# A transformer block's input projection: half of its contraction by one Strassen level, and indexer scores at full array height

## The chip, the cores and the metric

The kernel runs on 1 core of one Trainium2 chip. The metric is the device time of one execution in microseconds (us), here the median of three runs. TensorE multiplies matrices out of SBUF into PSUM (8 banks of 128 x 512 floats); VectorE and ScalarE compute on SBUF and PSUM; GpSimd and SyncE mostly issue DMAs. SBUF has 128 partitions.

## The reference

x is 512 tokens of 4096 features, all float32. The block computes

```
h  = RMSNorm(x) * pre_norm
z  = h @ w_in                       # 4096 -> 9808 columns, split into:
     q 2048 | c 512 | qi 1024 | k_idx 64 | w_idx 16 | gate_a 2048 | pool_in 2048 | gate_b 2048
c  = RMSNorm(c); k_idx = LayerNorm(k_idx)
I[t,s] = sum over 16 heads of w_idx[t,h] * relu(qi[t,h] . k_idx[s])   # heads of 64 features
top 128 keys per query of I, within admissible 64-token chunks
ya = softmax(q_lat . c_sel / sqrt(128)) . c_sel, 16 heads, mapped by w_uk and w_uv; times silu(gate_a)
yb = (trailing mean over 2/4/8/16 tokens - token) @ w_pool * pool_scale; times silu(gate_b)
out = x + RMSNorm(concat(ya, yb) @ w_out) * post_norm
```

Every large product is done in three matmuls of a reduced-precision format: each operand is split into a high part `hi` (a cast) and a low part `lo` (the rest), and hi*hi + hi*lo + lo*hi is accumulated.

## The kernel before

*Tiling.* h transposed is held in SBUF as 32 contraction tiles of 128 features x 512 tokens, each as a high and a low part (128 KB of a partition's memory). A **group** (function `group`, L254) makes 128 columns of z, transposed: 128 columns x 512 tokens in one PSUM bank. It loops over 8 quarters q of w_in's column block; each quarter is a 256 KB DMA of four 128 x 128 weight tiles, split by `staged` (L69: DMA on SP's queue, cast on ScalarE L66, subtraction on VectorE L67, rings of 4 buffers), and 4 x 3 matmuls (`mm3`, L78 to L82) of 512 columns. A group is 96 matmuls. Two PSUM banks ("acc") alternate between groups; six others ("w") serve everything else. There are 72 groups: 8 for qi, 16 each for pool_in, gate_b, q and gate_a. c, k_idx and w_idx come out of the first stage.

*Order of stages.* (0) L139: x is loaded, scaled and split, with c and k_idx beside it. (1) L298: 8 qi groups of 384 columns (the first 128 queries need no selection); `dots` (L299) makes the indexer scores of a group's two heads for 3 query blocks, each head on 64 of the array's rows (L307), relu on ScalarE, a weighted sum on VectorE. (2) L484: `pool_group` 0 (four pool_in groups with `mixer`, four gate_b groups, the pool map `ymix`); the top-k selection `select` (L335) goes on beside it on VectorE. (3) L492: 16 attention heads: a q group, a gate_a group, and `attn` (L495). (4) L563: `pool_group` 1 to 3. (5) L611: output projection, 20 of 32 contraction tiles by one Strassen level: 8 column blocks x 10 tile pairs = 80 steps; each forms seven weight combinations in `weights` (L384, VectorE and ScalarE), runs 7 products x 2 halves x 3 matmuls of 256 columns (L616 to L621), and after ten steps `collect` (L578) combines the seven products into partial sums, written to DRAM by GpSimd's queue. (6) L680: the remaining 12 tiles directly, added to the partials, norm and residual. Operands of stage 5 are read back from DRAM (`cat`) and formed by `operands` (L368) during the last groups.

*What sets the order.* Background work (dots, select, mixers, pool maps, attention) is written as Python generators in a queue `Bg` (L275) with priorities. `bg.step(per)` runs `per` pieces, one `yield` each; a group calls it after each of its first 7 quarters and once after its evacuation. `bg.drain` runs all that is left. A list scheduler then places the instructions on the engines' queues by this written order, later ones first where an earlier one is not ready or finds no free buffer. A buffer tag with `bufs=1` is taken by the next tile only when all readers of the last one are done; in `attn` these are the keys `kh`, `kl`, the queries `qh`, `ql`, the probabilities `prob` and the scratch `t2`; the gate `sg` has two.

Of the kernel before, what the change touches and what calls it, by code (L numbers as in the profile page):

```python
# [16 lines left out]
P = 128  # L17
# [31 lines left out]
def block_kernel(ctx: ExitStack, tc: tile.TileContext, xT, x, gk, wc, wkw, wf, wuk, wuv, kvn,  # L49
# [4 lines left out]
    big_a = ctx.enter_context(tc.tile_pool(name="big_a", bufs=1))  # L54
    big_stack = ctx.enter_context(ExitStack())
    big_b = big_stack.enter_context(tc.tile_pool(name="big_b", bufs=1))
    st_stack = ctx.enter_context(ExitStack())
    st = st_stack.enter_context(tc.tile_pool(name="st", bufs=4))
# [41 lines left out]
    slots = {}  # L100

    def big(t, shape, name, dt=F32R):
        return (big_b if t < NT else big_a).tile(shape, dt, tag=f"k{t}", name=name)

    def x_slot(i):
        t, j = divmod(i, 7)
        if t not in slots:
            slots[t] = big(t, [P, min(7, 2 * NK - 7 * t), S], f"xk{t}")
        return slots[t][:, j]

    xh, xl = [], []
# [13 lines left out]
    mb = cTp.tile([P, OFF[4]], F32, name="mb")  # L125
# [5 lines left out]
    with tc.tile_pool(name="s0", bufs=2) as s0:  # L131
# [7 lines left out]
        for k2 in range(NK // 2):  # L139
# [20 lines left out]
            for j in range(2):  # L160
# [3 lines left out]
                xh.append(x_slot(2 * k))  # L164
                xl.append(x_slot(2 * k + 1))
# [27 lines left out]
    isc = kixp.tile([P, OFF[4]], F32, name="isc")  # L193
# [60 lines left out]
    def group(gi, evac, per=1, t0=0, before=None, after=None):  # L254
        gis, evacs = (gi, evac) if isinstance(gi, tuple) else ((gi,), (evac,))
        zs = [bank("acc") for _ in gis]
        for q in range(8):
            for i, z in enumerate(zs):
                hi, lo = staged(wf[gis[i], q])
                if before:  # L260
                    before(q, i)
                for j in range(4):
                    k = 4 * q + j
                    mm3(z[:, t0:], (hi[:, ts(j, P)], lo[:, ts(j, P)]), (xh[k][:, t0:], xl[k][:, t0:]),
                        k == 0, k == NK - 1)
                if q < 7:
                    bg.step(per)
            if after:
                after(q)
            if q == 7:  # L270
                for z, evac in zip(zs, evacs):
                    evac(z)
                    bg.step(per)
# [24 lines left out]
    with tc.tile_pool(name="ix", bufs=2, reuse_waits="tile") as ix:  # L298
        def dots(g, qp):  # L299
            for b in range(1, NB):  # L300
                n = P * (b + 1)
                dp = [bank() for _ in range(2)]
                lhs = [sub(qp, slice(64 * j, 64 * j + 64), ts(b, P)) for j in range(2)]
                rhs = [sub(kT, slice(64 * j, 64 * j + 64), slice(0, n)) for j in range(2)]
                for i, (x0, x1) in enumerate(((0, 0), (0, 1), (1, 0))):
                    for j in range(2):
                        nc.tensor.matmul(dp[j][:, :n], lhs[j][x0], rhs[j][x1], start=i == 0, stop=i == 2)  # L307
                yield
                for j in range(2):
                    h = 2 * g + j  # L310
                    r = ix.tile([P, S], F32, name="relu")
                    A.activation(r[:, :n], dp[j][:, :n], AF.Relu)
                    o = isc[:, OFF[b]:OFF[b + 1]]
                    w = wix[:, b, h:h + 1]
                    if h == 0:
                        V.tensor_scalar(o, r[:, :n], w, None, op0=ALU.mult)
                    else:
                        V.scalar_tensor_tensor(o, r[:, :n], w, o, op0=ALU.mult, op1=ALU.add)
                yield

        for g in range(8):
            qp = (ix.tile([P, S], F32R, name="qih"), ix.tile([P, S], F32R, name="qil"))
# [10 lines left out]
    kT_stack.close()  # L333

    def select():  # L335
        V.memset(mb[:, :P], 0.0)
        V.memset(mb[:CHUNK, CHUNK:P], NEG)
        for b in range(1, NB):
            V.memset(isc[:CHUNK, OFF[b + 1] - CHUNK:OFF[b + 1]], INADM)
        yield  # L340
        for r in range(TOPK // 8):
            for b in range(1, NB):
                o = isc[:, OFF[b]:OFF[b + 1]]
# [5 lines left out]
        for b in range(1, NB):  # L349
            V.tensor_scalar(mb[:, OFF[b]:OFF[b + 1]], isc[:, OFF[b]:OFF[b + 1]], -3.2e38, NEG,  # L350
# [17 lines left out]
    def operands(i, pool, tag, bufs, home):  # L368
        w = pool.tile([P, 8, H], F32, tag=tag, name="cw", bufs=bufs)
        q, s = w[:, 0:4], w[:, 4:8]  # L370
        for j in range(2):
            nc.sync.dma_start(q[:, 2 * j:2 * j + 2], cat[i + KA * j].rearrange("p (a t) -> p a t", a=2))
# [5 lines left out]
        o = home([P, 2, 7, H], f"ops{i}")  # L378
        split(w[:, 0:3:2], o[:, 0, 0:2], o[:, 1, 0:2])
        split(w[:, 3:8], o[:, 0, 2:7], o[:, 1, 2:7])  # L380
        ops[i] = o
        yield

    def weights(db, i):  # L384
        w = ow.tile([P, 8, H], F32, tag="wr", name="wr", bufs=2)
        nc.sync.dma_start(w[:, 0:4], wq[i, db].rearrange("p (a c) -> p a c", a=4))
        V.tensor_sub(w[:, 4:6], w[:, 1:3], w[:, 0:2])  # L387
        V.tensor_sub(w[:, 6], w[:, 2], w[:, 4])
        V.tensor_sub(w[:, 7], w[:, 3], w[:, 6])
        hi = ow.tile([P, 7, H], F32R, tag="wh", name="wh", bufs=2)  # L390
        lo = ow.tile([P, 7, H], F32R, tag="wl", name="wl", bufs=2)
        split(w[:, 0:3:2], hi[:, 0:2], lo[:, 0:2])
        split(w[:, 3:8], hi[:, 2:7], lo[:, 2:7])
        return hi, lo
# [4 lines left out]
    def pool_group(pl, pm, g):  # L399
# [22 lines left out]
        for c in range(4):  # L422
            def evac(z, c=c):
# [4 lines left out]
            group(G_PI + 4 * g + c, evac)  # L428
# [7 lines left out]
        def gated(d, yp):  # L436
            def evac(z):
                bg.drain(1)
# [9 lines left out]

        if g < 3:
            for d in range(4):  # L450
                group(G_GB + 4 * g + d, add(d), 2 if d == 0 else 1)
            return lambda: None
        evs = [add(d) for d in range(4)]
        group(G_GB + 4 * g, evs[0], 2)
        bg.drain(1)

        def rest():
            first = []

            def early(q):  # L460
                if q == 3:
                    first.append(operands(0, ow, "wr", 2, lambda sh, n: ex.tile(sh, F32R, name=n)))
                if q in (3, 5):
                    next(first[0])

            group(G_GB + 4 * g + 1, evs[1], after=early)
            cur = []

            def before(q, i):
                if i == 0:  # L470
                    cur[:] = [operands(q, ow, "wr", 2, lambda sh, n: big(q - 1, sh, n))] if q else []
                for e in cur:
                    next(e)

            def after(q):
                if q == 7:
# [3 lines left out]
            group((G_GB + 4 * g + 2, G_GB + 4 * g + 3), (evs[2], evs[3]), before=before, after=after)  # L480
# [11 lines left out]
    with tc.tile_pool(name="at", bufs=1, reuse_waits="tile") as at:  # L492
# [53 lines left out]
        for h in range(NH):  # L546
# [14 lines left out]
    cT_stack.close()  # L561
    right = ctx.enter_context(ExitStack())
    with tc.tile_pool(name="pl1", bufs=1, reuse_waits="tile") as pl:  # L563
        with tc.tile_pool(name="pm1", bufs=1, reuse_waits="tile") as pm:
            for g in range(1, 4):
                rest = pool_group(pl, pm, g)
        ex = right.enter_context(tc.tile_pool(name="ex", bufs=1, side="right", reuse_waits="tile"))
# [3 lines left out]

    inner.close()
    st_stack.close()

    PRODUCTS = ((0, 0), (1, 2), (4, 5), (5, 4), (3, 3), (2, 6), (6, 1))
# [21 lines left out]

    def load_cat(e):
        raw = st.tile([P, S], F32, tag="raw", name="cat_raw")
        nc.sync.dma_start(raw, cat[2 * KA + e])  # L600
        ct[e] = (fin.tile([P, S], F32R, name=f"ch{e}"), fin.tile([P, S], F32R, name=f"cl{e}"))
        split(raw, *ct[e])

    def prefetch(n):
        if n < len(steps) and n not in ahead:
# [3 lines left out]
            ahead[n] = staged(wout[lanes[lane][0], e])  # L609

    for n, (db, i) in enumerate(order):  # L611
# [12 lines left out]
        if db == 0 and i in (0, 1, 3, 4):  # L624
            if i in (0, 3):
                late = [operands(8 + i // 3, oc, "cw", 1, lambda sh, m, t=7 + i // 3: big(t, sh, m))]
            next(late[0])
        if db == 7:
            if i == NT:
                big_stack.close()  # L630
                fin_stack = ctx.enter_context(ExitStack())
                fin = fin_stack.enter_context(tc.tile_pool(name="fin", bufs=1, reuse_waits="tile"))
                st = fin_stack.enter_context(tc.tile_pool(name="st2", bufs=4, reuse_waits="tile"))
            if i > KA - 3:
                prefetch(i - KA + 2)
        if i == KA - 1:
            pt = oc.tile([P, 7, 512], F32, name="pt")
# [12 lines left out]
    def spare(i):  # L650
        t, j = NT + i // 7, i % 7
        if t not in home:
            home[t] = big(t, [P, 7, 512], f"sp{t}", F32)
# [68 lines left out]
def _lay_out(x, pre_norm, w_in, kv_norm, w_uk, w_uv, idx_k_norm_g, idx_k_norm_b, w_pool, pool_scale, w_out,  # L722
# [16 lines left out]
    def quads(m):  # L739
# [6 lines left out]
    inv = np.stack([1.0 / np.minimum(pos, n) for n in WINS]).astype(np.float32).reshape(1, -1)  # L746
    a = {
# [5 lines left out]
        "wf": np.concatenate([groups(part[i]) for i in (2, 6, 7, 0, 5)]),  # L753
# [31 lines left out]
```

## Time and profile before

| | |
|---|---|
| runs shown | 2581.66, 2585.19, 2586.48 us; median 2585.19 |
| profiled execution | 2583.32 us, span from first to last instruction 2581.5 |
| mean granted TensorE clock | 0.997 |
| instructions | 34385, of them 13210 matmuls |
| HBM | 291.43 MB read, 25.17 MB written |

The page gives each engine's busy time and its share of the span (PE: matmuls, PEld: weight loads, DVE: VectorE, ACT: ScalarE, POOL: GpSimd). Matmuls are pipelined: one lasts longer than the distance to the next start, so distances are read from a timeline. A line number may be a helper's (L66, L67, L80 to L82). In a table of windows each row has the stretch and its length, then busy us and number of instructions of PE, PEld, DVE, ACT and POOL, the granted clock (1.00 is 2.4 GHz, 0.50 is 1.2 GHz), the DMA share and GB/s. In a timeline a row has start, duration, engine, line, operation, out<-in, shapes and count; brackets hold the idle time before it and what ended it. In groups by line "| busy us, mean ns of one | idle us before <-what ended it".

### The profile page before, as it was taken

How to read it: one execution, taken by the hardware profiler on the slowest of the kernel's cores; microseconds unless marked ns; L12 is line 12 of the kernel's file. 1: busy time of each engine (PE TensorE's matmuls, PEld its weight loads, DVE VectorE, ACT ScalarE, POOL GpSimd, SP SyncE). 2: the span in 40 equal slices, each digit the busy share in tenths (PEclk: the TensorE clock that was granted, in tenths of full speed). 3: DMA queues.
4: the chain of work that ended last, by engine and by line, in shares of the span. 5: the costliest groups of instructions: out<-in, count | busy, mean ns of one | idle time of the engine just before them, and what ended most of it. 6: DMA issues, size and time to landing. Idle time of an engine off the chain costs nothing.

```text
span 2581.5 us, 34385 instructions
## 1 busy us (share of the span) xinstructions
PE 2549.7 (99%) x13210; PEld 2187.5 (85%) x13210; DVE 1340.4 (52%) x2376; ACT 901.0 (35%) x1558; POOL 13.3 (1%) x28
## 2 busy tenths in 40 slices
PE   9999999999999999999999999999999999999996
PEld 7899888888888888888888888888899999998875
DVE  6465863343444444444344334334687777763447
ACT  6444322232333333333332222222444444443333
POOL 0000000000000000000000000000000000000000
PEclk9999999999999999999999999999999999999998
DMA  8433233322332232323333332332443433476456
GB/s 307 149 111 109 92 102 106 102 91 94 93 96 90 90 97 92 94 91 93 94 94 95 106 106 94 110 102 94 157 130 132 128 117 127 135 248 225 136 174 238
DMA packets 163077, 318.86 MB, mean 124 GB/s; under 512 B 18528, under 2 KB 26848, under 8 KB 162912
## 3 DMA queue, kind: packets, MB, share of 16 engines
q1 hardware_dynamic: 160480, 308.28, 37.5%
q0 software_dynamic: 2432, 8.39, 0.8%
q8 instruction: 103, 1.69, 0.3%
q14 instruction: 62, 0.51, 0.1%
HBM read 291.43 MB, written 25.17 MB: 123 GB/s over the span
## 4 chain that ended last, share of the span: by engine, by line
PE 94%; DVE 3%; DMA 2%; ACT 1%; issue 0%; SPq 0%; DVEq 0%; ACTq 0%
PE ps_acc L80 21%; PE ps_acc L82 20%; PE ps_acc L81 20%; PE ps_w L81 6%; PE ps_w L82 6%; PE ps_w L80 6%; PE ps_w L620 4%; PE ps_w L621 4%; PE ps_w L619 4%; DMA raw<-in_wout 1%; PE ps_w L535 1%; PE ps_w L307 1%; PE ps_acc L621 1%; DMA wr<-in_wq 1%; PE ps_acc L620 1%; PE ps_acc L619 1%
## 5 line engine op out<-in xcount | busy, mean ns | idle before, releaser
L67 DVE TENSOR_TENSOR lo<-raw,hi 128x512 fp32r<-128x512 f32 x776 | 533.6, 690 | 934.6 <-ACT hi L66 861.7
L66 ACT CAST hi<-raw 128x512 fp32r<-128x512 f32 x776 | 482.0, 622 | 1254.8 <-PE ps_acc L81 910.7
L80 PE MATMUL ps_acc<-xk,hi 128*128 128x512 f32 (+1 forms) x2304 | 893.0, 388 | 0.0
L82 PE MATMUL ps_acc<-xk,lo 128*128 128x512 f32 (+1 forms) x2304 | 883.7, 384 | 0.1
L81 PE MATMUL ps_acc<-xk,hi 128*128 128x512 f32 (+1 forms) x2304 | 883.6, 384 | 0.0
L80 PEld LDWEIGHTS ps_acc<-xk,hi 128*128 128x128 f32 x2304 | 432.8, 188 | 81.7 <-issue 2.5
L82 PEld LDWEIGHTS ps_acc<-xk,lo 128*128 128x128 f32 x2304 | 432.5, 188 | 81.6 <-DVE lo L67 0.4
L81 PEld LDWEIGHTS ps_acc<-xk,hi 128*128 128x128 f32 x2304 | 433.0, 188 | 76.1
L620 PE MATMUL ps_w<-wl,ops 128*128 128x256 f32 x960 | 270.4, 282 | 3.2 <-DVE wl L67 3.2
L621 PE MATMUL ps_w<-wh,ops 128*128 128x256 f32 x960 | 270.6, 283 | 0.0
L619 PE MATMUL ps_w<-wh,ops 128*128 128x256 f32 x960 | 268.8, 282 | 0.5 <-DVE sg L363 0.5
L66 ACT CAST wh<-wr 128x512 fp32r<-128x512 f32 (+1 forms) x160 | 145.3, 942 | 223.7 <-PE ps_acc L621 181.0
L67 DVE TENSOR_TENSOR wl<-wr,wh 128x512 fp32r<-128x512 f32 (+1 forms) x160 | 173.8, 1089 | 48.1 <-ACT wh L66 47.4
L620 PEld LDWEIGHTS ps_w<-wl,ops 128*128 128x128 f32 x960 | 181.6, 189 | 4.3 <-DVE wl L67 4.0
L619 PEld LDWEIGHTS ps_w<-wh,ops 128*128 128x128 f32 x960 | 180.2, 189 | 0.7 <-DVE sg L363 0.7
L621 PEld LDWEIGHTS ps_w<-wh,ops 128*128 128x128 f32 x960 | 180.5, 188 | 0.0
L81 PE MATMUL ps_w<-lo,ch 128*128 128x512 f32 x312 | 122.9, 394 | 5.1 <-DVE lo L67 5.0
L80 PE MATMUL ps_w<-hi,ch 128*128 128x512 f32 x312 | 120.9, 392 | 1.9 <-ACT hi L66 1.9
L82 PE MATMUL ps_w<-hi,cl 128*128 128x512 f32 x312 | 121.9, 391 | 0.0
L81 PEld LDWEIGHTS ps_w<-lo,ch 128*128 128x128 f32 x312 | 59.0, 189 | 20.0 <-DVE lo L67 7.9
L80 PEld LDWEIGHTS ps_w<-hi,ch 128*128 128x128 f32 x312 | 58.7, 189 | 15.2 <-ACT hi L66 3.2
L387 DVE TENSOR_TENSOR wr<-wr 128x512 f32<-128x512 f32 x80 | 55.2, 690 | 28.8 <-DMA wr<-in_wq 28.4
(215 smaller groups left out, 2278.3 us busy)
## 6 DMA issues: line engine op xcount, KB each, us to landing
raw<-in_wf SPq DMA_DIRECT2D x576, 256.0 KB, 2.6
wr<-in_wq SPq DMA_DIRECT2D x80, 512.0 KB, 3.6
raw<-in_wout SPq DMA_DIRECT2D x120, 256.0 KB, 3.5
raw<-in_wc SPq DMA_DIRECT2D x32, 256.0 KB, 5.3
xn<-in_x SPq DMA_DIRECT2D x32, 256.0 KB, 4.5
pp<-part SPq DMA_DIRECT2D x32, 256.0 KB, 4.6
xt<-in_xT SPq DMA_DIRECT2D x15, 512.0 KB, 5.5
cw<-cat SPq DMA_DIRECT2D x20, 256.0 KB, 3.0
```

What stands on the lines that cost most here:

```text
L66: A.copy(hi, src)
L67: V.tensor_sub(lo, src, hi.bitcast(F32))
L80: nc.tensor.matmul(dst, lh, rh, start=start, stop=False)
L81: nc.tensor.matmul(dst, lh, rl, start=False, stop=False)
L82: nc.tensor.matmul(dst, ll, rh, start=False, stop=stop)
L307: nc.tensor.matmul(dp[j][:, :n], lhs[j][x0], rhs[j][x1], start=i == 0, stop=i == 2)
L387: V.tensor_sub(w[:, 4:6], w[:, 1:3], w[:, 0:2])
L535: nc.tensor.transpose(tp[:, ts(b - s, P)], prob[:, OFF[b] + P * s:OFF[b] + P * s + P], ident)
L619: nc.tensor.matmul(zz, ab[0], wh[:, w], start=i == 0 and h == 0, stop=False)
L620: nc.tensor.matmul(zz, ab[0], wl[:, w], start=False, stop=False)
L621: nc.tensor.matmul(zz, ab[1], wh[:, w], start=False, stop=i == KA - 1 and h == 1)
```

## The change

*SBUF and order.* x's tiles 0 to 15 live in eight tiles `p0` to `p7` by quadrants (two contraction halves x two halves of the tokens), tiles 16 to 31 in `d0` to `d7`. After the qi groups the first four gate_b groups run in full, interleaved, and their raw results go to DRAM (`zxd`). During the qi groups `d0` to `d7` are copied to DRAM (`xsp`); then x is read again and its sums for Strassen are formed in their place (`build`).

*The new stage.* The 60 remaining groups, in 30 pairs, get contraction tiles 0 to 15 by one Strassen level: per pair 4 steps; a step loads 512 KB, forms seven weight combinations (`form_weights`, the body of the former `weights`), and runs 2 x 7 x 3 matmuls of 256 columns with the weights stationary and x moving. After four steps ScalarE copies four half-filled or full banks and `collect_z` combines them into the pair's partial sums, which GpSimd's queue writes to DRAM (`zpd`). In the last pair `p0` to `p7` are refilled with tiles 16 to 31 from `xsp`. Then the staging rings are opened again on the side where the combination buffers were.

*The direct stages.* `group` now loads a partial sum into one of 8 slots (`d6`, `d7`), runs 16 tiles (4 quarters, 48 matmuls), and adds the partial on VectorE before the old evacuation. Background work is stepped after 3 quarters and once after the evacuation. `pool_group` 0 runs its four pool_in groups interleaved, and its gates (from `zxd`) as background; pool groups 0, 1 and 2 precede attention, 3 follows. After attention the staging rings move to the space that the latent `cTh`, `cTl` and attention's tiles leave. The output's operands are formed in two parts (`sum_part`, `pure_part`), and the tail rotates its buffers within the same tiles; its work is the same.

*The scores.* A head's query high and low parts are stacked on the 128 rows (the other head's rows hold the low part), the keys are there twice already, and a block takes 2 heads x 2 matmuls of 128 rows in place of 2 x 3 of 64.

```diff
 def dots(g, qp):
     for b in range(1, NB):
         ...
-        lhs = [sub(qp, slice(64 * j, 64 * j + 64), ts(b, P)) for j in range(2)]
-        rhs = [sub(kT, slice(64 * j, 64 * j + 64), slice(0, n)) for j in range(2)]
-        for i, (x0, x1) in enumerate(((0, 0), (0, 1), (1, 0))):
-            for j in range(2):
-                nc.tensor.matmul(dp[j][:, :n], lhs[j][x0], rhs[j][x1], start=i == 0, stop=i == 2)
+        for j in range(2):
+            for i in range(2):
+                nc.tensor.matmul(dp[j][:, :n], qp[j][:, ts(b, P)], kT[i][:, :n], start=i == 0, stop=i == 1)
...
 def evac(z, qp=qp):
     ...
-    split(qf[:, P:], *sub(qp, slice(None), slice(P, S)))
+    for j in range(2):
+        o, r = (slice(IDX_D * i, IDX_D * i + IDX_D) for i in (j, 1 - j))
+        split(qf[o, P:], qp[j][o, P:], qp[j][r, P:])
-group(G_QI + g, evac, t0=P)
+stream(wf, (g,), FULL, (evac,), t0=P)
+nc.gpsimd.dma_start(xsp[g], xd[g])
...
+def stream(src, gis, ks, evac, per=1, t0=0, tags=None, before=None, after=None):
+    zs = [bank(t) for t in tags or ["acc"] * len(gis)]
+    for q in range(len(ks) // 4):
+        for i, z in enumerate(zs):
+            hi, lo = staged(src[gis[i], q])
+            ...
+            for j in range(4):
+                k = ks[4 * q + j]
+                mm3(z[:, t0:], (hi[:, ts(j, P)], lo[:, ts(j, P)]), (xh[k][:, t0:], xl[k][:, t0:]),
+                    k == ks[0], k == ks[-1])
+            if 4 * q + 4 < len(ks):
+                bg.step(per)
+        ...
+    for z, e in zip(zs, evac):
+        e(z)
+        bg.step(per)
+def group(gi, evac, per=1, **kw):
+    ...
+        nc.sync.dma_start(parts[-1], zpd[g])
+    def adder(zp, e):
+        def run(z):
+            V.tensor_add(zp, z, zp)
+            e(zp)
+        return run
+    stream(wd, gis, DIRECT, [adder(*a) for a in zip(parts, evacs)], per, **kw)
...
+def collect_z(m, pt):
+    V.tensor_add(pt[:, 1], pt[:, 0], pt[:, 1])
+    V.tensor_add(pt[:, 2], pt[:, 2], pt[:, 0])
+    V.tensor_add(pt[:, 4], pt[:, 4], pt[:, 2])
+    yield
+    V.tensor_add(pt[:, 0], pt[:, 3], pt[:, 4])
+    V.tensor_add(pt[:, 3], pt[:, 3], pt[:, 2])
+    V.tensor_add(pt[:, 3:5], pt[:, 3:5], pt[:, 5:7])
+    yield
+    z = [zpd[2 * m + j].rearrange("p (a t) -> p a t", a=2) for j in range(2)]
+    nc.gpsimd.dma_start(z[0], pt[:, 1:4:2])
+    nc.gpsimd.dma_start(z[1][:, 0], pt[:, 4])
+    nc.gpsimd.dma_start(z[1][:, 1], pt[:, 0])
+    yield
+with tc.tile_pool(name="pa", bufs=2, side="right", reuse_waits="tile") as pa:
+    for n, (m, t) in enumerate(order_s):
+        if t == 0:
+            banks = [bank(b) for b in ("w", "w", "w", "acc")]
+        wh, wl = first.pop(n)
+        for c in range(2):
+            i = 2 * t + c
+            for j, (a, w) in enumerate(PRODUCTS):
+                ...
+                nc.tensor.matmul(zz, w0, x0, start=i == 0 and j % 2 == 0, stop=False)
+                nc.tensor.matmul(zz, w1, x0, start=False, stop=False)
+                nc.tensor.matmul(zz, w0, x1, start=False, stop=last)
+            if m == NPAIR - 1:
+                xd[i] = big(f"p{i}", [P, 2, 2, S], f"xr{i}")
+                nc.gpsimd.dma_start(xd[i], xsp[i])
+                ...
+        if t == NA // 2 - 1:
+            pt = pa.tile([P, 7, H], F32, name="pt")
+            ...
+            bg.add(collect_z(m, pt), 0)
+        if n + 2 < len(order_s):
+            first[n + 2] = s_weights(n + 2)
+        bg.step()
+    bg.drain()
+wa_stack.close()
+st_stack = ctx.enter_context(ExitStack())
+st = st_stack.enter_context(tc.tile_pool(name="st", bufs=4, side="right", reuse_waits="tile"))
...
-    pool_group(pl, pm, 0)
+    for g in range(3):
+        pool_group(pl, pm, g)
     bg.drain()
...
-    group(G_Q + h, evac)
+    group(Q + h, evac)
     sg = at.tile([P, S], F32, tag="sg", name="sga", bufs=2)
     bg.add(attn(h, qp, sg))
-    group(G_GA + h, lambda z, sg=sg: gate(at, z, sg))
+    group(GA + h, lambda z, sg=sg: gate(at, z, sg))
 bg.drain()
 cT_stack.close()
+st_stack.close()
+st = st_stack.enter_context(tc.tile_pool(name="st3", bufs=4, reuse_waits="tile"))
...
-    for g in range(1, 4):
-        rest = pool_group(pl, pm, g)
+    rest = pool_group(pl, pm, 3)
+    bg.drain(3)
```

## Rows read from the trace of the kernel before

**Rows 1.** The page: busy time by engine; the last chain by engine.

```profile
PE 2549.7 (99%) x13210; PEld 2187.5 (85%) x13210; DVE 1340.4 (52%) x2376; ACT 901.0 (35%) x1558; POOL 13.3 (1%) x28
...
PE 94%; DVE 3%; DMA 2%; ACT 1%; issue 0%; SPq 0%; DVEq 0%; ACTq 0%
```

**Rows 2.** Table of windows: output's Strassen stage, direct projection.

```profile
1889.00:2292.00 403.00, 400.99 (x3334) 400.04 (x3334) 321.57 (x460) 178.09 (x226) 11.45 (x21) 1.00 0.42 134
1330.00:1870.00 540.00, 540.00 (x2378) 446.06 (x2377) 227.14 (x376) 146.69 (x233) 0.00 (x0) 1.00 0.34 108
```

**Rows 3.** Timeline of PE, direct projection, 107 steps apart.

```profile
461.98 0.39 PE L80 MATMUL ps_acc<-xk,hi 128*128 128x512 f32 x1
...
486.23 0.39 PE L82 MATMUL ps_acc<-xk,lo 128*128 128x512 f32 x1
```

**Rows 4.** Timeline of PE, output's Strassen stage, 54 steps apart.

```profile
2029.79 0.28 PE L619 MATMUL ps_w<-wh,ops 128*128 128x256 f32 x1
...
2036.27 0.28 PE L619 MATMUL ps_w<-wh,ops 128*128 128x256 f32 x1
```

**Rows 5.** Timeline of PE around one block of indexer scores.

```profile
228.16 0.34 PE L82 MATMUL ps_acc<-xk,lo 128*128 128x384 f32 x1
...
228.42 0.50 PE L307 MATMUL ps_w<-kTh,qih 64*128 64x512 f32 x2
...
229.60 0.33 PE L81 MATMUL ps_acc<-xk,hi 128*128 128x384 f32 x1
```

**Rows 6.** Groups by line and form: weight forming, output stage.

```profile
L67 DVE TENSOR_TENSOR wl<-wr,wh 128x1280 fp32r<-128x1280 f32 x80 | 119.0, 1488 | 15.4 <-ACT wh L66 15.1
...
L66 ACT CAST wh<-wr 128x1280 fp32r<-128x1280 f32 x80 | 101.0, 1263 | 27.7 <-DVE wr L389 27.6
...
L387 DVE TENSOR_TENSOR wr<-wr 128x512 f32<-128x512 f32 x80 | 55.2, 690 | 28.8 <-DMA wr<-in_wq 28.4
...
L67 DVE TENSOR_TENSOR wl<-wr,wh 128x512 fp32r<-128x512 f32 x80 | 55.2, 690 | 32.6 <-ACT wh L66 32.3
...
L66 ACT CAST wh<-wr 128x512 fp32r<-128x512 f32 x80 | 49.6, 620 | 196.0 <-PE ps_acc L621 181.0 <-DMA wr<-in_wq 7.9 <-PE ps_w L621 3.9
...
L388 DVE TENSOR_TENSOR wr<-wr 128x256 f32<-128x256 f32 x80 | 33.7, 422 | 1.3
```

**Rows 7.** Waits (us in total, times, longest), output's Strassen stage.

```profile
PE ps_w L620 <- DVE wl L67: 2.0, 3, 1.1
```

**Rows 8.** DMA issues (count, KB each, us to landing).

```profile
wr<-in_wq SPq DMA_DIRECT2D x80, 512.0 KB, 3.6
...
part<-pt POOLq DMA_DIRECT2D x16, 256.0 KB, 3.2
```

**Rows 9.** Table of windows, attention, from one head's transposes to the next's.

```profile
1218.50:1269.83 51.33, 51.33 (x240) 42.82 (x239) 21.09 (x43) 16.52 (x33) 0.00 (x0) 1.00 0.31 93
```

**Rows 10.** Groups by line and form in the same head's window.

```profile
L67 DVE TENSOR_TENSOR lo<-raw,hi 128x512 fp32r<-128x512 f32 x17 | 11.7, 691 | 23.5 <-ACT hi L66 21.2 <-PE ps_w L535 2.3
...
L514 ACT ACTIVATE prob<-prob,nm 128x512 f32<-128x512 f32 x1 | 0.7, 724 | 1.4 <-DVE nm L511 1.4
...
L511 DVE CUSTOM_DVE_ANT_0 prob<-ps_w,mb 128x512 f32<-128x512 f32 x1 | 0.7, 683 | 0.0
...
L516 DVE TENSOR_SCALAR prob<-prob,sm 128x512 f32<-128x512 f32 x1 | 0.5, 485 | 0.0
```

**Rows 11.** Timeline of PE at the end of attention's last head.

```profile
1324.87 0.82 PE L535 MATMUL ps_w<-ident,prob 128*128 128x128 f32 x6
...
1325.44 0.47 PE L80 MATMUL ps_acc<-xk,hi 128*128 128x512 f32 x1
...
1329.07 0.28 PE L82 MATMUL ps_w<-pth,vl 128*128 128x128 f32 x1
```

**Rows 12.** Timeline of PE behind an idle stretch of the tail.

```profile
2536.92 0.79 PE L81 MATMUL ps_w<-lo,ch 128*128 128x512 f32 x1 [2.71 <-DVE lo L67]
```

**Rows 13.** Table of windows, the two us behind that row.

```profile
2538.00:2540.00 2.00, 2.00 (x6) 1.59 (x5) 2.00 (x5) 0.00 (x0) 0.00 (x0) 0.50 0.90 306
```

More of the change, by code (lines that the diff above doesn't have):

```diff
@@ L252, in block_kernel @@
         split(tp, *kT)
[L254 to L257, printed above, removed]
+    FULL = list(range(2 * NA, NK)) + list(range(2 * NA))
+    DIRECT = FULL[:NK - 2 * NA]
+    def stream(src, gis, ks, evac, per=1, t0=0, tags=None, before=None, after=None):
+        zs = [bank(t) for t in tags or ["acc"] * len(gis)]
+        for q in range(len(ks) // 4):
             for i, z in enumerate(zs):
-                hi, lo = staged(wf[gis[i], q])
+                hi, lo = staged(src[gis[i], q])
                 if before:
@@ new lines, in block_kernel, with before, after @@
+        builds = [e for e in range(NA) for _ in range(2)]
+        gens = {}
+        def before(q, i):
+            if q >= 2 and i % 2 == 0 and builds and not (q > 5 and i):
+                for _ in range(2 if q < 4 else 1):
+                    pass
+            if q >= 2 and builds:
+                e = builds.pop(0)
+                if e not in gens:
+                    gens[e] = build(e)
+                next(gens[e])
+        def after(q):
+            if q == 0:
+                bg.drain()
+                ix_stack.close()
+                kT_stack.close()
+                lend["w1"] = wa_stack.enter_context(tc.tile_pool(name="wa1", bufs=1, reuse_waits="tile"))
+                lend["bs"] = bs_stack.enter_context(tc.tile_pool(name="bs", bufs=1, side="right", reuse_waits="tile"))
+            if q == 7:
+                first[0] = s_weights(0)
@@ new lines, in keep, with evac, s_weights @@
+        def keep(d):
+            def evac(z):
+                raw = st.tile([P, S], F32, tag="raw", name="zx")
+                A.copy(raw, z)
+                nc.gpsimd.dma_start(zxd[d], raw)
+            return evac
+        order_s = [(m, t) for m in range(NPAIR) for t in range(NA // 2)]
+        first = {}
+        def s_weights(n):
+            m, t = order_s[n]
+            raw = lend["w1"].tile([P, 8, H], F32, tag="wr", name="wr", bufs=2)
+            nc.sync.dma_start(raw[:, 0:4], ws[m, t].rearrange("p (a c) -> p a c", a=4))
+            return form_weights(raw, lend["w2"] if n % 2 else lend["w1"])
@@ L427, in evac @@
                 bg.add(mixer(z, c), 0)
-            group(G_PI + 4 * g + c, evac)
+            return evac
+        if g == 0:
+            group(tuple(PI + c for c in range(4)), [taker(c) for c in range(4)], tags=("acc", "acc", "w", "w"))
+        else:
+            for c in range(4):
+                group(PI + 4 * g + c, taker(c), 5 if c == 0 and g == 1 else 1)
         def ymix(d, yp):
@@ L752, in _lay_out @@
         "wkw": rows(w[:, o[3]:o[5]]),
-        "wf": np.concatenate([groups(part[i]) for i in (2, 6, 7, 0, 5)]),
+        "wf": np.concatenate([qi, gb[:ONCE]])[:, [4, 5, 6, 7, 0, 1, 2, 3]],
+        "ws": quad,
+        "wd": rest[:, 4:],
         "wuk": np.asarray(w_uk)[0].reshape(NH, NC, P, DH).transpose(0, 2, 1, 3).reshape(NH, P, LAT),
```

303 lines of the change are left out of this document (209 added, 94 removed).

## The prediction, made before the change was run

> **What bounds the kernel now.** The page's busy line comes first: TensorE is busy 99% of 2581.5 us, and 94% of the chain that ended last is matmuls [rows 1]. So the time is the matmuls' number times their spacing, plus a few gaps. The table of windows says where other engines come near: in the direct input projection VectorE is busy 42%, in the Strassen stage of the output projection 80%, and even there TensorE is idle only 2 of 403 us; the granted clock is 1.00 in both [rows 2]. A busy matmul's own duration is no spacing (they overlap), so spacings are read from starts. 512 columns: 107 steps between the two starts shown, 24.25 us, 0.2266 us each [rows 3]. 256 columns: 54 steps, 6.48 us, 0.1200 us each [rows 4]. Half the columns cost 53%, not 50%: about 13 ns per matmul do not shrink.
>
> The sums below are made against the profiled execution, 2583.3 us (span 2581.5); the median of the runs shown is 2585.2, so 1.9 us are added at the end.
>
> **1. The Strassen stage, -47.9 us.** 60 of the 64 groups behind the indexer's lose 16 of their 32 contraction tiles: 60 x 16 x 3 = 2880 matmuls of 512 columns, 2880 x 0.2266 = 652.7 us. Added: 30 pairs x 8 tile pairs x 7 products x 3 = 5040 matmuls of 256 columns, 5040 x 0.1200 = 604.8 us. All are on TensorE, which sets the time. Seven eighths of the columns would be 12.5%; the 13 ns leave 7.3%.
>
> The Trainium skill, "TensorE: Matmul & The Clock Gate", section "Back-to-back issue gap", gives N/2.4 + 2.5 ns; by it the stage would save 71 us. The trace does not agree: 226.6 and 120.0 ns, 11 ns more than its 215.8 and 109.2. The rows decide; the rule is a rival below.
>
> **2. Indexer scores, -5.7 us.** Before, a block's six matmuls on 64 rows start two at a time: three slots [rows 5]. The count alone says three slots become four full ones, so dearer: the three blocks of a group have 256, 384 and 512 columns, slots of 0.120, 0.173 (halfway between the two spacings) and 0.227 us, 0.52 in all; +4.2 us over 8 groups. But the entry and exit cost: from the last full-height start before (228.16) to the second one after (229.60) pass 1.44 us. Two 384-column spacings of 0.173 off leave 1.09 us for 3 x 0.227 = 0.68 us of columns, 0.41 us more. Per group before: 3 x 0.520 + 3 x 0.41 = 2.79 us; after: 4 x 0.520 = 2.08 us, if full height has no such entry. One of the 24 blocks is shown. 8 x 0.71 = 5.7 us. Bounds: -5.7, and +4.2 if the 0.41 us are a wait for operands and stay. Of the skill, "TensorEngine Tiling (Array Packing)", two rules pull apart here: section "Theoretical Speedup" has two 64-row tiles run at once, which speaks for the old form, and "Key Properties" says a change of tiling mode drains the engine, which speaks for the new. The trace shows both, pairs that start together and 0.41 us around them, and by its numbers the second weighs more.
>
> The query evacuation now splits twice on 64 rows, one more low part of 384 columns on VectorE beside the next group's 96 x 0.173 = 16.6 us of matmuls: nothing; uncovered it would delay a block by 0.6. The 8 spills of 1 MB and 4 raw sums go by GpSimd's queue beside matmuls: nothing.
>
> **3. Feeding the Strassen stage, +3 us (0 to 18).** A step is 42 matmuls, 5.04 us, like one of the output stage, with the same load and weight forming: 0.69 + 2 x 0.42 + 0.69 + 1.49 = 3.71 us of VectorE, and 1.9 us of ScalarE [rows 6]. The combination of the seven products comes every 4 steps, at half width: 5 x 0.42 + 0.69 = 2.8 us, 0.70 per step, so 4.41 of 5.04 us, 88% (the output stage: 80%). The raw buffer's loop, load 3.6 [rows 8], three subtractions 1.5, casts and low parts 3.5, is 8.6 of the 10.1 us that two buffers give; a combination of up to 1.5 us fits only just. In the output stage the low part was late 3 times, 2.0 us [rows 7], over 8 combinations of double width. 30 half-width ones at 0.1 us: 3. At 0.6 us (one VectorE burst without slack) they are 18.
>
> **4. Handover to the direct stage, +10.5 us (2 to 18).** The staging buffers were given away and return where the combination buffers lie, so the first direct group's weights cannot all be staged ahead. Behind the last matmul come: a ScalarE copy 0.6, the combination 2.8, a write by GpSimd's queue 3.2 [rows 8], then cast and low part 1.3: 7.9 us, and I add 1.1 because 8 MB of x tiles are reloaded at the time. Behind the waiting staging stand only the four part loads on SP's queue. After an idle 2.71 us the trace resumes at a granted clock of 0.50 (1.2 GHz) [rows 12, 13] for some 3 us: seven matmuls at twice the spacing, 1.5 us lost; the idle time here is longer, so the same 1.5. Low: the buffers happen to be free (2). High: the raw buffers wait too, and a slow load (5.5) and more clock are added (18).
>
> **5. Attention's cover, +17 us (8 to 52).** This decides. A head's background work has 12 pieces, every fourth head's 16: 208. A group offers a place for one piece behind each block of four tiles: 8 before, 4 now. After the first query group 31 groups give 124 places; 84 pieces, 6.7 heads, are left when the last group is done. The eight slots for partial sums let groups run four heads ahead, so nothing stops this earlier. Up to there TensorE stays dense as now. The remainder runs without cover. TensorE per head: 51.33 us between the same events of two heads [rows 9] less 192 x 0.2266 = 43.5: 7.8 us; one value computation (48 x 0.2266 = 10.9) falls in it: 6.7 x 7.8 + 10.9 = 63 us. VectorE per head: 21.1 [rows 9] less 11.7 for 17 low parts [rows 10], plus 0.7 for its own weight: 10.1; with 8 x 0.69 for the values: 6.7 x 10.1 + 5.5 = 73 us. So at least 10 us are idle. The order is no strict queue: before, next-group matmuls already run between the last head's transposes and products [rows 11], so heads will overlap. I add 1 us a head for latency: 17. Low: 8, when the next pool group fills the end. High: nothing overlaps: keys 2.7 and their split 1.3; softmax 5 (the last block's 0.68, 0.72 and 0.49 [rows 10] with small ones 2.3, the three narrower ones ahead of it 3 by estimate); transposes 0.8; the first split and product 1.5; the other three 4.2 [rows 11]: 15.5 us a head, 7.7 idle, 6.7 x 7.7 = 52.
>
> **6. Elsewhere, +2 us (-1 to 6).** The sum of 60 partials costs VectorE 0.69 us each beside 10.9 us of matmuls: nothing. Top-k, VectorE work alone, now has twenty groups of 10.9 us ahead of attention: nothing; uncovered it would hold attention's first mask. At the output stage's start one more half operand (0.42 + 0.69 us of VectorE) is formed beside steps where VectorE is at 80% or more, and the last pool group forms its operands in half the matmul time: +2. The tail is as before.
>
> **Sum.** 2583.3 - 47.9 - 5.7 + 3 + 10.5 + 17 + 2 = 2562.2; with 1.9: 2564 us.
>
> **Rivals.**
> *Gaps filled.* The list order finds other work: terms 3 to 6 at their low ends, 0 + 2 + 8 - 1: 2540.6, 2541 rounded. For it: the interleaving of [rows 11], 100% busy windows today. Against: the freed staging space ties the next groups to the old buffers. 0.17.
> *Attention's remainder runs as a chain.* Place: the last 6.7 heads, whose keys, queries and probabilities have one buffer each. Price 52 instead of 17: 2599, slower. It turns to slower from 5.7 us idle per head (38 us in all). For it: single buffers and three-instruction round trips. Against: VectorE needs 10.1 of 15.5 us, and keys can be computed ahead. 0.12.
> *VectorE binds the new stage.* Each pair's combination pushes the low parts by 0.5 to 1.5 us: 30 x that less the 3 counted: 2576 to 2606, middle 2591. For it: 88% busy, a buffer loop with 1.5 us of slack. Against: 80% left 2 us idle in 403. 0.12.
> *Spacing by columns.* The 13 ns are not per matmul in the new stage, where x moves and weights stand: saving 71, 2541. Against: two long runs of starts. That is what the skill's gap rule would make. 0.02.
> That the work is not removed is excluded: the matmul counts are written out.
>
> **How the numbers follow.** My case: 0.57, 2552 to 2578. Changes within 0.2% (5.2 us, 2580.0 to 2590.4) are what a measurement of this kernel can't tell from none. Faster: 0.56 of my case, 0.17, 0.02, and 0.03 of the VectorE case: 0.78. Same: 0.01 of mine, 0.05 of the VectorE case, 0.02 of the chain case: 0.08. Slower: the rest, 0.14. The range 2540 to 2598 leaves out the chain's worse half, the worst VectorE stretch and the best fills.
>
> **What would show it.** Starts of the new stage 0.120 us apart and 42 in 5.0 us; a block of dots in four single slots with no 0.4 us around; one idle stretch of about 9 us at the handover with the clock at 0.5 behind it; transposes of the last six or seven heads without group matmuls between, 10 to 11 us apart. Wrong: steps over 5.4 us, TensorE dense to the end of attention, or heads 15 us apart.

## The result, and the profile after

The change made the kernel slower: 2648.2 us (2646.6 to 2649.4, four runs) against 2584.4 (2581.7 to 2586.5, four runs), ratio 1.0247, 95% interval 1.0229 to 1.0265. 2564 was predicted. The profiled execution took 2648.1 us, its span is 2646.4.

The page of after, its busy line and the row of granted clock in 40 slices (the line answers to [rows 1]):

```profile
PE 2554.5 (97%) x15322; PEld 2267.3 (86%) x15322; DVE 1718.2 (65%) x3034; ACT 1046.7 (40%) x1724; POOL 77.6 (3%) x138
...
PEclk9999999999999999999999999988999999999998
```

VectorE went from 52% to 65% and TensorE still shows 97%, so shares say little here: the idle 1% became 3%, and one place near two thirds of the span runs below full clock. The timelines of PE say where the 64.9 us are: the stages, taken from starts of their first and last matmuls, in us:

```
                                         before    after   difference
stage 0                                   117.0    121.0      +4.0
indexer groups and 4 gate groups          248.1    247.4      -0.7
tiles 0 to 15 of the other 60 groups      652.7    607.7     -45.0   (before: 2880 x 0.2266)
TensorE idle at the handover                0.0     17.3     +17.3
direct tiles, attention, pool maps        865.6    950.7     +85.1
output projection, Strassen stage         408.5    412.0      +3.5
the rest                                  289.6    290.3      +0.7
```

The new stage gives what was promised; the direct part behind it loses twice that. Windows of after, in time order (columns as in [rows 2]):

```profile
50.00:80.00 30.00, 30.00 (x130) 23.22 (x129) 15.43 (x28) 17.16 (x38) 2.81 (x5) 1.00 0.99 374
```

```profile
400.00:900.00 500.00, 499.07 (x4202) 498.65 (x4201) 409.46 (x651) 227.65 (x300) 44.47 (x75) 1.00 0.40 133
...
980.00:990.00 10.00, 0.00 (x0) 0.00 (x0) 0.00 (x0) 0.00 (x0) 0.93 (x2) 0.58 1.06 408
990.00:1000.00 10.00, 6.57 (x18) 5.21 (x19) 3.31 (x5) 3.06 (x5) 0.00 (x0) 0.57 0.68 243
...
993.40:1709.40 716.00, 715.97 (x3162) 580.07 (x3162) 353.77 (x672) 225.52 (x414) 0.00 (x0) 1.00 0.37 113
```

```profile
1709.40:1841.90 132.50, 98.82 (x409) 71.62 (x407) 78.26 (x208) 51.16 (x123) 0.00 (x0) 0.84 0.19 59
```

Between 50 and 80, still in stage 0, GpSimd already issues spills and the DMA engines are full (0.99; before 0.84 there); TensorE does not wait yet. The new stage is dense (499 of 500 us) with VectorE at 82%. At 980 to 990 TensorE does nothing while the DMA engines are full. Up to 1709 it is dense again; then follow 132.5 us in which one group is left: busy 98.8, mean clock 0.84.

Spacing: the timeline of PE in after, 54 steps of 256 columns in the new stage, and 107 steps of 512 columns in the direct stage (they answer to [rows 4] and [rows 3]):

```profile
400.10 0.28 PE L488 MATMUL ps_w<-xs,wh 128*128 128x256 f32 x1
...
406.51 0.28 PE L488 MATMUL ps_w<-xp,wh 128*128 128x256 f32 x1
...
1000.08 0.40 PE L82 MATMUL ps_acc<-xr,hi 128*128 128x512 f32 x1
...
1025.15 0.39 PE L84 MATMUL ps_w<-xr,lo 128*128 128x512 f32 x1
```

6.41 / 54 = 0.1187 us; 25.07 / 107 = 0.2343 us, at a clock of 1.00, where before had 0.2266 with the same shapes. That was in no term of the prediction.

The handover, and attention's remainder with its last group and the first transposes of its last heads, PE in after (brackets: idle time, and what ended it):

```profile
993.43 0.80 PE L82 MATMUL ps_acc<-xr,hi 128*128 128x512 f32 x1 [17.04 <-ACT hi L68]
...
1719.92 0.78 PE L82 MATMUL ps_acc<-xr,hi 128*128 128x512 f32 x1
...
1732.07 0.39 PE L84 MATMUL ps_acc<-xr,lo 128*128 128x512 f32 x1
...
1740.46 0.40 PE L84 MATMUL ps_w<-kh,ql 128*128 128x512 f32 x1
1742.73 0.44 PE L733 MATMUL ps_w<-ident,prob 128*128 128x128 f32 x1 [1.87 <-DVE prob L714]
...
1746.23 0.80 PE L82 MATMUL ps_w<-pth,vh 128*128 128x512 f32 x1 [0.73 <-ACT pth L68]
...
1755.14 0.91 PE L82 MATMUL ps_w<-kh,qh 128*128 128x128 f32 x4 [0.96 <-ACT kh L68]
...
1759.40 0.30 PE L733 MATMUL ps_w<-ident,prob 128*128 128x128 f32 x1 [1.87 <-DVE prob L714]
...
1784.78 0.60 PE L733 MATMUL ps_w<-ident,prob 128*128 128x128 f32 x4
...
1797.02 0.30 PE L733 MATMUL ps_w<-ident,prob 128*128 128x128 f32 x1 [1.87 <-DVE prob L714]
...
1813.02 0.30 PE L733 MATMUL ps_w<-ident,prob 128*128 128x128 f32 x1 [1.87 <-DVE prob L714]
...
1828.68 0.30 PE L733 MATMUL ps_w<-ident,prob 128*128 128x128 f32 x1 [1.15 <-DVE sm L713]
...
1841.86 0.79 PE L82 MATMUL ps_acc<-xr,hi 128*128 128x512 f32 x1 [4.50 <-ACT hi L68]
```

A head waits at each link of its chain (keys, softmax, transposes, their split). The last group runs from 1719.92 to 1732. Behind it come the transposes of six heads, 16.7, 25.4, 12.2, 16.0 and 15.7 us apart, with no group matmul between; the 25.4 hold the value computation, which every fourth head has. At the end stands a stall of 4.5 us where the staging ring (the four buffers each of `raw`, `hi` and `lo`) is moved. Why the handover lasts shows in SP's queue in after, and in that queue's own waits from 965 to 1000 (us in total, times, longest):

```profile
973.94 2.81 SPq L304 DMA_DIRECT2D zt<-zpd  x5
976.80 1.38 SPq L641 DMA_DIRECT2D zt<-zxd  x3
982.49 17.74 SPq L74 DMA_DIRECT2D raw<-in_wd  x9
```

```profile
SPq L74 <- DMA zt<-zpd: 10.1, 4, 4.3
```

The loads of the partials stand ahead of the first raw weights. They start at 973.94 and 976.43, when the last Strassen matmuls leave their slots `d6` and `d7`. The first four raw loads then wait until a partial has landed, one for each: the first partial lands at 982.43, 8.5 us after its issue, and the first raw load goes out at 982.49. It lands 10.2 us later.

### The profile page after: what moved, and what is told of

Same layout as the page of the kernel before. It is cut to its first block, busy times and chain, and to the rows that moved or that the text cites. A ratio compares the mean times of both kernels' runs of the same rounds, so it can differ in the third digit from the quotient of the medians.

```text
span 2646.4 us, 39505 instructions
## 1 busy us (share of the span) xinstructions
PE 2554.5 (97%) x15322; PEld 2267.3 (86%) x15322; DVE 1718.2 (65%) x3034; ACT 1046.7 (40%) x1724; POOL 77.6 (3%) x138
## 5 line engine op out<-in xcount | busy, mean ns | idle before, releaser
L68 ACT CAST wh<-wr 128x512 fp32r<-128x512 f32 (+1 forms) x400 | 362.1, 943 | 488.0 <-PE ps_acc L488 265.6
L69 DVE TENSOR_TENSOR lo<-raw,hi 128x512 fp32r<-128x512 f32 x416 | 286.1, 689 | 396.3 <-ACT hi L68 396.0
L69 DVE TENSOR_TENSOR wl<-wr,wh 128x512 fp32r<-128x512 f32 (+1 forms) x400 | 434.9, 1088 | 122.4 <-ACT wh L68 120.3
L68 ACT CAST hi<-raw 128x512 fp32r<-128x512 f32 x416 | 257.1, 619 | 614.5 <-PE ps_acc L83 417.9
L82 PE MATMUL ps_acc<-xr,hi 128*128 128x512 f32 x928 | 373.6, 403 | 21.5 <-ACT hi L68 21.5
L83 PE MATMUL ps_acc<-xr,hi 128*128 128x512 f32 x928 | 368.6, 397 | 0.0
L84 PE MATMUL ps_acc<-xr,lo 128*128 128x512 f32 x928 | 368.1, 397 | 0.0
L82 PEld LDWEIGHTS ps_acc<-xr,hi 128*128 128x128 f32 x928 | 176.5, 190 | 60.2 <-ACT hi L68 21.9
L83 PEld LDWEIGHTS ps_acc<-xr,hi 128*128 128x128 f32 x928 | 176.2, 190 | 38.5
L487 PE MATMUL ps_w<-xp,wl 128*128 128x256 f32 x720 | 203.8, 283 | 5.4 <-DVE wl L69 5.3
L486 PE MATMUL ps_w<-xp,wh 128*128 128x256 f32 x720 | 203.2, 282 | 0.0
L488 PE MATMUL ps_w<-xp,wh 128*128 128x256 f32 x720 | 203.2, 282 | 0.0
L488 PE MATMUL ps_w<-xs,wh 128*128 128x256 f32 x720 | 203.1, 282 | 0.0
L486 PE MATMUL ps_w<-xs,wh 128*128 128x256 f32 x720 | 202.8, 282 | 0.0
```

What stands on the lines that cost most here:

```text
L68: A.copy(hi, src)
L69: V.tensor_sub(lo, src, hi.bitcast(F32))
L82: nc.tensor.matmul(dst, lh, rh, start=start, stop=False)
L83: nc.tensor.matmul(dst, lh, rl, start=False, stop=False)
L84: nc.tensor.matmul(dst, ll, rh, start=False, stop=stop)
L486: nc.tensor.matmul(zz, w0, x0, start=i == 0 and j % 2 == 0, stop=False)
```

## The experiments

Theory after the result: four causes. Attention pieces left without cover, that is, without group matmuls that fill TensorE while a head waits (e2); the place of the staging ring in SBUF, which the change moved to the right end, 32 bytes beside a multiple of 64 (e1, e5, e6, e8); SP's order and the reload at the handover (e3, e4); and scores that save less than thought (e9). The rivals are in the expectations. All times are medians; "less" is against after, ratios are against before.

**e2, pieces at half quarters.**

```diff
                         k == ks[0], k == ks[-1])
+                    if half and j == 1:
+                        bg.step()
...
-            group(Q + h, evac)
+            group(Q + h, evac, half=True)
...
-            group(GA + h, lambda z, sg=sg: gate(at, z, sg))
+            group(GA + h, lambda z, sg=sg: gate(at, z, sg), half=True)
```

> The changed kernel in which the attention groups hand out one attention piece after every second contraction tile, not after every fourth, so that a head has 16 places and not 8. Theory (pieces without cover run as a chain): the 132 us behind the last group of the attention stage, 63 us of them TensorE work, go; that work comes back between the matmuls of the groups, and 2648 falls to 2585 to 2600. Rival (the pieces wait for VectorE and ScalarE wherever they stand): new waits between the quads take back what the end loses, 2630 to 2650.

2598.8 us, 49.4 less; ratio 1.0064 (1.0049 to 1.0079). Window and timeline of PE in e2, through attention and at its end:

```profile
1300.00:1790.00 490.00, 489.67 (x2267) 392.95 (x2267) 269.06 (x577) 182.47 (x382) 0.00 (x0) 1.00 0.32 99
```

```profile
1790.87 0.28 PE L84 MATMUL ps_w<-pth,vl 128*128 128x128 f32 x1
...
1795.95 0.79 PE L82 MATMUL ps_acc<-xr,hi 128*128 128x512 f32 x1 [4.80 <-ACT hi L68]
```

Dense to the end, clock 1.00: with 16 places a head the chain's waits vanish under the groups' matmuls. VectorE at 55% doesn't bind. The stall where the ring moves stays, and is a cost of its own.

**e1, ring aligned, same place.** A pool with one tile of 32 bytes is opened on the right ahead of `st`.

> The changed kernel with a strip of 32 bytes per partition reserved at the right end of SBUF, so that the staged weight ring (raw, hi, lo) starts at a multiple of 64 bytes and no longer 32 bytes beside one; it stays in the same region, on the right. Theory (start address): the 512-column matmuls that read the ring, some 3800 of them, go from 0.2346 back to 0.2266-0.2275 us each; less those in the stretch where TensorE waits anyway, 2648 falls to about 2620 (2615 to 2628). Rival (the region or the distance between the ring and the x operands sets the spacing): 0.2346 stays and the time is 2645 to 2651.

2642.1 us, 6 less: my theory fell. PE, direct stage, 107 steps:

```profile
1001.22 0.40 PE L84 MATMUL ps_acc<-xr,hi 128*128 128x512 f32 x1
...
1026.18 0.39 PE L86 MATMUL ps_acc<-xr,lo 128*128 128x512 f32 x1
```

0.2333: 1.0 of the 7.7 ns lost came back. Aligned, but on the right, is not enough.

**e5 and e8, the same question asked of before.**

```diff
 # e5: 32 bytes ahead of the ring and 32 behind it, on the left
+    pad("pad0")
...
+        if len(pads) == 1:
+            pad("pad1")
...
 # e8: an aligned ring on the right
+    edge = ctx.enter_context(tc.tile_pool(name="edge", bufs=1, side="right"))
+    nc.vector.memset(edge.tile([P, 8], F32, name="edge"), 0.0)
-    st = st_stack.enter_context(tc.tile_pool(name="st", bufs=4))
+    st = st_stack.enter_context(tc.tile_pool(name="st", bufs=4, side="right"))
...
```

> The kernel before, with 32 bytes per partition ahead of the staged weight ring and 32 behind it: the ring stays on the left, where it was, but starts 32 bytes beside a multiple of 64, as it does in the changed kernel; nothing else moves. The ring aligned on the right (e1) brought only some 1.2 ns a matmul in the direct stage, so theory (the place sets the spacing, the offset a little): some 6900 matmuls of 512 columns by 1.2 ns, 2584 becomes 2592 (2587 to 2600). Rival (the offset matters where the ring is on the left): 0.2268-0.2280 becomes 0.234, +45 us, 2620 to 2635.

> The kernel before, with the staged weight ring at the right end of SBUF (start a multiple of 64 bytes), until the last pool group, where a ring on the left is opened as in the changed kernel; the other small tiles move down by its size. Theory (the place of the ring sets the spacing): some 6300 matmuls of 512 columns go from 0.2278 to 0.2305-0.2335 us, 384-column ones stay at 0.1735, the last pool group stays at 0.2267; 2584 becomes 2617 (2610 to 2625). Rival (something else in the changed kernel slows them: reloads, partials, VectorE): spacing stays, 2580 to 2590.

e5: 2624.0 us, ratio 1.0158 (1.0143 to 1.0173), the rival's figure. e8: 2615.0 us, 1.0124 (1.0109 to 1.0139), as the theory had it; but e8's ring is on the left again from the three pool groups behind attention on, so some 4650 matmuls were touched, not 6300. PE, 107 steps each; e5:

```profile
300.19 0.40 PE L90 MATMUL ps_acc<-xk,hi 128*128 128x512 f32 x1
...
325.15 0.40 PE L89 MATMUL ps_acc<-xk,hi 128*128 128x512 f32 x1
```

and e8, before and behind the return to the left:

```profile
300.07 0.39 PE L82 MATMUL ps_acc<-xk,hi 128*128 128x512 f32 x1
...
325.04 0.40 PE L84 MATMUL ps_acc<-xk,lo 128*128 128x512 f32 x1
...
1400.14 0.39 PE L84 MATMUL ps_acc<-xk,lo 128*128 128x512 f32 x1
...
1424.39 0.39 PE L83 MATMUL ps_acc<-xk,hi 128*128 128x512 f32 x1
```

0.2333 in e5; 0.2334 and then 0.2266 in e8, within one run. Each alone, 32 bytes of offset or the right end, costs 6.7 ns a matmul; both together (after) 7.7. The Trainium skill, "SBUF — State Buffer", section "Operand start alignment", asks only that an operand start at a multiple of its element size, and calls that legality, not speed; e5 shows that 32 bytes are worth 41 us to this kernel.

**e6, sides swapped.** Every pool but the x operands goes to the other side, so the ring stands where before has it.

> The changed kernel with all pools but the x operands on the other side of SBUF: the staged weight ring now stands on the left, right behind the x operands, at the addresses that it has in the kernel before; what was on the left is on the right. Theory (the place of the ring): 512-column spacing in stage 0, the 4 groups done in full and the direct stage goes from 0.2343 to 0.2266-0.228 us, but the last pool group's ring, now on the right, to 0.234; 2648 becomes 2622 (2615 to 2630). Rival (not the place, but what else the changed kernel does): 2643 to 2651.

2624.8 us, 23.4 less; 1.0157 (1.0140 to 1.0174). PE, direct stage, 107 steps, 0.2266 again:

```profile
990.06 0.39 PE L83 MATMUL ps_acc<-xr,hi 128*128 128x512 f32 x1
...
1014.31 0.39 PE L82 MATMUL ps_w<-xr,hi 128*128 128x512 f32 x1
```

Behind 1200 the mean is 0.230, for the groups' own matmuls too, although the ring is still on the left. Latents and keys are on the right now; whether that is the reason is not shown. So the 23.4 us are not all the ring's in the direct tiles: in the profiles 12.5 come from there up to attention's end, 4.5 from the new stage (its spacing is 0.1173 here), 2.4 from the groups ahead of it, 2.2 from the output's stage, and the last pool group, whose ring is on the right now, loses 1.6.

**e3 and e4, the handover.**

```diff
 # e3
-            nc.sync.dma_start(parts[-1], zpd[g])
+            nc.gpsimd.dma_start(parts[-1], zpd[g])
...
-                    nc.sync.dma_start(z, zxd[d])
+                    nc.gpsimd.dma_start(z, zxd[d])
 # e4
-                    xd[i] = big(f"p{i}", [P, 2, 2, S], f"xr{i}")
-                    nc.gpsimd.dma_start(xd[i], xsp[i])
...
-                        xh[2 * NA + 2 * i + j], xl[2 * NA + 2 * i + j] = xd[i][:, j, 0], xd[i][:, j, 1]
+                        xh[2 * NA + 2 * i + j], xl[2 * NA + 2 * i + j] = x_slot(i + NA * j)
```

> The changed kernel with the loads of the Strassen partials (zt from zpd and zxd) issued on GpSimd's queue, no longer on SyncE's ahead of the first raw weights. Theory (SyncE stands at the partials, whose buffers are released by the last Strassen matmuls, and the raw weights stand behind them): TensorE's idle time at the handover falls from 17.2 to 6 to 10 us, and the time to about 2639 (2636 to 2643). Rival (the 8 MB that are reloaded fill the DMA engines): idle time stays at 15 to 18 us, 2645 to 2651.

> The changed kernel without the reload of the 16 direct tiles (8 MB): the direct stage multiplies the 16 tiles of the Strassen stage a second time instead, so its sums are others, with the same instructions on TensorE. Theory (SyncE's order): the raw weights are still issued only after the last Strassen matmuls, but land in 3 us and not 10; idle time 17.2 to 8 to 11 us, time 2640 to 2643. Rival (the reload's bandwidth alone): idle time falls to 2 to 4 us, time 2631 to 2635.

e3: 2642.4 us, 5.8 less; e4: 2638.2, 10.0 less. PE, e3:

```profile
975.78 0.28 PE L488 MATMUL ps_acc<-xs,wh 128*128 128x256 f32 x1
984.84 0.80 PE L82 MATMUL ps_acc<-xr,hi 128*128 128x512 f32 x1 [8.78 <-ACT hi L68]
...
990.04 0.80 PE L84 MATMUL ps_acc<-xr,lo 128*128 128x512 f32 x1 [3.98 <-DVE lo L69]
```

and e4:

```profile
971.79 0.28 PE L488 MATMUL ps_acc<-xs,wh 128*128 128x256 f32 x1
980.49 0.79 PE L82 MATMUL ps_acc<-xp,hi 128*128 128x512 f32 x1 [8.42 <-ACT hi L68]
...
983.19 0.79 PE L84 MATMUL ps_acc<-xp,lo 128*128 128x512 f32 x1 [1.48 <-DVE lo L69]
```

17.0 us idle became 12.8 and 9.9. Neither story alone holds: with the order mended the first raw load still takes 8.2 us beside 8 MB, and without the 8 MB some 10 us stay. The two causes feed each other: without the 8 MB the first partial lands after 2.6 us, and no raw load waits for a partial. A third layer shows in e10.

**e9, scores alone, on before.** The diff of `dots` and the evacuation, as in the change.

> The kernel before with only its indexer scores made full-height (q in two half-zeroed tiles, no row tiling), as in the changed kernel; the rest is that of before. Theory (step 2 of the prediction: each of 24 blocks loses the entry and exit of row tiling): 5.7 us less, 2583 becomes 2578 (2575 to 2580). Rival (the time of the block hides behind VectorE, which is busy all through that stage in the trace of before): 2582 to 2585.

2581.0 us against 2582.4, ratio 0.9994 (0.9985 to 1.0003): no difference that can be told. PE in before around a group's first block, from the last start ahead of it to the second behind it, and the same in e9:

```profile
198.72 0.34 PE L82 MATMUL ps_acc<-xk,lo 128*128 128x384 f32 x1
198.98 0.38 PE L307 MATMUL ps_w<-kTh,qih 64*128 64x256 f32 x2
...
199.81 0.34 PE L81 MATMUL ps_acc<-xk,hi 128*128 128x384 f32 x1
```

```profile
197.60 0.34 PE L82 MATMUL ps_acc<-xk,lo 128*128 128x384 f32 x1
...
197.93 0.28 PE L305 MATMUL ps_w<-kTl,qi 128*128 128x256 f32 x1
198.29 0.39 PE L305 MATMUL ps_w<-kTh,qi 128*128 128x256 f32 x1
...
198.80 0.34 PE L81 MATMUL ps_acc<-xk,hi 128*128 128x384 f32 x1
```

Less two spacings of 384 columns (0.347 us), as step 2 counts, the blocks of 256, 384 and 512 columns take 0.75, 0.92 and 1.09 us in before, 2.77 a group, and 0.86, 0.70 and 0.93 in e9, 2.48 (all groups but the first and last). Row tiling's entry and exit cost 0.39 to 0.41 us in all three, as step 2 read them. What it had wrong is the other side: a group's first full-height block takes 0.86 where four spacings are 0.48. Its third matmul starts 0.36 us behind the second; why is not shown. By the trace some 2.3 us are saved over eight groups, which the medians can neither show nor exclude.

**e7 and e10, put together.** e7: e2's, e3's and e6's edits, and 32 bytes reserved at the right end. e10 adds a ring that stays on the left (no move before the last pool group), output weights on the right, and four reloads that wait:

```diff
+    def late(q):
+        if q < 2:
+            reload(4 + 2 * q, True)
+            reload(5 + 2 * q, True)
...
-    st_stack.close()
-    st = st_stack.enter_context(tc.tile_pool(name="st3", bufs=4, side="right", reuse_waits="tile"))
```

> The three together: sides swapped (with 32 bytes reserved at the right end, so that the pools there start at multiples of 64 bytes), attention pieces after every second contraction tile, partials loaded on GpSimd's queue. If the three causes are apart, their gains add: 2648 less 49 (e2) less 6 (e3) less some 26 (place of the ring) gives 2567 (2560 to 2575), under the 2584 of the kernel before. Rival (they overlap: with faster matmuls there is less cover for the attention pieces): 2575 to 2590.

> As e7, with three more edits: the small constants and the staged ring stand on the left for the whole kernel, so the ring is not moved before the last pool group; the output stage's weights stand on the right, at multiples of 64 bytes, as in e8; four of the eight reloads wait until the direct stage's first raw weights have landed. From e7's 2571: the stall of 4.9 us at the move of the ring goes; the handover's 9.9 us become 4 to 6; the output stage takes 404 us as in e8 and not 410. Together 2555 (2548 to 2562). Rival (the stalls are given back where the next buffer is late, and the output stage's spacing hangs on more than the start address): 2564 to 2574.

e7: 2571.2 us, ratio 0.9955 (0.9940 to 0.9969): faster than before, and the three gains nearly add (49.4 + 5.8 + 23.4 = 78.6; 77.0 measured), though it is no clean sum: with the 32 bytes the new stage's spacing is 0.1159, where e6 had 0.1173. e10: 2559.8 us (2552.6 to 2564.0), 0.9908 (0.9892 to 0.9924), the fastest version; its profiled execution took 2552.6. In e10's window from the first direct matmul to attention's end TensorE never rests:

```profile
974.74:1755.00 780.26, 780.11 (x3556) 636.02 (x3557) 430.92 (x864) 273.37 (x536) 31.12 (x57) 1.00 0.39 120
```

The stall of the move is gone, and the output's Strassen stage takes 407 us (404 expected). The handover still idles 8.7 us where 4 to 6 were expected. Waits in e10 there (us in total, times, longest):

```profile
ACT hi L66 <- DMA zpd<-pt: 7.5, 1, 7.5
```

That is the third layer: the new ring lies on the last pair's combination buffer, and the cast waits until that partial is written out. The prediction priced this one; it put 1.1 us on the reload and nothing on the order.

## Why the prediction was wrong, step by step

*Step 1 and 3, the new stage: right.* Predicted 604.8 + 3 = 607.8 us, measured 607.7, but the close hit is luck, two errors that cancel: the spacing is 0.1187 and not 0.1200 (5040 x 0.1187 = 598.3), and 9.5 us of waits stand where 3 were set. Some 7 of them are one stall at 378, 4.4 us idle for the second step's low part, and half clock behind it. VectorE at 82% did not bind. The rival *Spacing by columns* (109.2 ns) is refuted by 118.7.

*Step 5, attention's cover: the step that failed.* "I add 1 us a head for latency: 17." Its count was nearly right: 6.7 heads predicted, and the transposes of six fall behind the last group, those of a seventh just ahead of it. Its overlap was not: no group matmul is left to fill in, the heads come 17.2 us apart in the mean (12 to 17, and 25 with the values), where 10 to 11 was forecast and the chain rival had 15.5, and the clock falls to a mean of 0.84 through the waits. e2 prices it: 49.4 us, near the chain rival's 52, not 17. That rival had 0.12. [rows 11] had misled me: matmuls of the next group filled in there because the next group had not yet run, and in the remainder none was left.

*Step 4, the handover: too small.* 10.5 predicted, 18 the upper bound; 17.0 idle plus 2.3 for twelve matmuls at half clock, 0.43 us apart. The combination buffer made up most of the sum. The reload (e4) was priced at 1.1, and the part loads were thought to stand behind the staging on SP's queue; they stood ahead (e3).

*Step 2, scores:* -1.4 with an interval of -3.9 to +0.8, not -5.7. The 0.41 us were read rightly, but full height was given no loss of its own, and a group's first block has one of 0.38 (e9). The spills, "nothing" in this step, are scheduled into stage 0, where TensorE now waits between 94 and 101 us; about 2 of that stage's 4.0 us are starts over 0.3 us apart.

*What no step held.* Every term took 0.2266 us for matmuls that the change leaves as they are. They cost 0.2343 in the direct part as long as the ring is on the right. By count and spacing, an estimate, that is 23 us on some 3000 matmuls there, some 2 of the 4.0 in stage 0, and 3 in the four full groups. Swapping the sides (e6), which puts other buffers on the right, returned 12.5 us there. The stall where the ring moves, 4.5, was not seen either (step 6).

In the direct part 85.1 us are thus: cover 48.1 (e2's own timeline), spacing 23 by that estimate, the ring's move 5, half clock 2.3; 7 are not assigned. Of the 84 us between 2564 and 2648 some 31 are step 5's (48 in place of 17), some 28 the place of the ring by count, 9 the handover's. With the cover mended (e2) the time is still 2598.8, 0.6% slower than before: the place of the ring is the second large part of the miss.

## What to carry to other kernels

When a stage is shortened, count what ran hidden under it, and look for new places before the work is done: half as many matmuls per group needed twice as many hand-out points, and their lack alone was 49 us. Price a handover by everything queued ahead of the first load and by all traffic beside it, not by the one buffer that comes to mind. When a change moves buffers, measure the spacing of untouched matmuls in one stage before anything else.

## What was not expected of the hardware

Spacing of 512-column float32r matmuls with the ring at four places: left, multiple of 64 bytes 0.2266 us; left, 32 beside 0.2333; right, multiple of 64 0.2333; right, 32 beside 0.2343. Matmuls of 384 columns kept 0.1735 to 0.1747 in all of these. The ring's place is not the whole of it: in e6, e7 and e10 the ring is on the left at a multiple of 64, and the direct stage behind 1200 still has a mean of 0.230. With 256 columns the output's Strassen stage went the other way in e8: 0.118 where weights on the right start at a multiple of 64, 0.120 in before. The mechanism stays open: a ring lower on the right, which would tell the side from the height of the address, was not tried.
